# Modulation rows in the weight-sum tiles, one a pair, and chunk 0 of the key and value activations prepared beside the query pairs

## The chip, the core and the metric

The kernel runs on one core of a Trainium2 chip. The core has five engines with instruction queues of their own: TensorE (PE in the profile, its weight loads are PEld), VectorE (DVE), ScalarE (ACT), GpSimd (POOL) and SyncE (SP, which here only issues DMAs). Each queue is worked off in order; an instruction whose semaphore is not there yet holds all behind it. The metric is the device time of one execution in microseconds. Three timed runs of the kernel before gave 2887.72, 2887.82 and 2893.54 us, median 2887.82.

## The reference

A decoder trunk of two layers on `x` (1024 tokens by 1024 channels, float32). Layer 0 mixes by causal pooling, layer 1 by dilated attention over keys and values projected from the stream after layer 0. Each layer ends in a gated FFN (1024 to 2 x 2816, a causal convolution over three tokens, SiLU gate, 2816 to 1024). Every sub-layer is normalised, scaled and shifted by modulation rows, and added back through a gate row. What matters here:

```python
cond = jax.nn.silu(c)
mod = cond @ ada_w[layer] + ada_b[layer]              # six rows of 1024 a layer
sh1, sc1, g1, sh2, sc2, g2 = jnp.split(mod, 6, axis=-1)
...
kv_shift, kv_scale = jnp.split(cond @ kv_ada_w + kv_ada_b, 2, axis=-1)
hkv = _modulate(_rmsnorm(x, kv_norm_g), kv_shift, kv_scale)
kv = (hkv @ w_kv).reshape(b, s, 2, N_BRANCHES, N_HEADS, HEAD_DIM)
...
h = _modulate(_rmsnorm(x, norm2_g[layer]), sh2, sc2)
x = x + g2[:, None, :] * _conv_ffn(h, ...)
```

So a modulation row of 1024 values is a product of a vector with a 1024 x 1024 matrix: 14 of them, 4 MB each.

## The kernel before

Activations lie transposed in SBUF, channels on partitions, tokens in two chunks of 512. Every float32 operand is split in a high part (written by ScalarE, L107, `whi`, `h`, `slab`) and a low part (VectorE subtracts, L108, `wlo`, `l`), and a product is three matmuls: high by high, high by low, low by high (L341 to L343, L415 to L417, L1012 to L1014).

The up projection of an FFN and the query projection run in **pairs** (`Pair`, 22 in an FFN, 12 for the queries) by a scheme of seven products of 2 x 2 blocks. For a pair, VectorE forms weight sums in two tiles of a pool `s` that has two places: `s21` (L455, L456) and `s34` (L460, L461), which are then split. The first eight pairs have two of their products made ahead and parked in DRAM (`ed`, L436); `rest` loads them back. `gate` (L492) evacuates the products, convolves (L504), and stores the row to `gd` by a DMA from GpSimd's queue (L533).

The down projection (`Ffn.down`, L549) goes through the 22 rows of `gd` in sets of three, the last of four. Each set loads its rows and weights through three places `wraw`, splits them, and walks eight row blocks by two chunks (`down_pieces`); VectorE adds each result to the stream tile `x` (L377). The last set (`down_last`, L382) also norms: chunk 0 is finished first, then `steps(0)` is advanced once per piece of chunk 1: its first step makes `nps` on TensorE, the square root chain and the diagonal `ndg` on VectorE (L207), the second the broadcast `nrs` on TensorE (L210), and the others scale one row block each (L222, L228). It has four call sites, one for each norm joint of the kernel: into the first FFN, into the query projection, into the second FFN, and into the output.

Modulation rows 0 to 4 are made early in other ways. Rows 5, 6, 7, 12, 13 come from `ada_dot` (L317) in the first FFN, rows 8 to 11 in the value projection: eight tiles `araw` of 512 KB a row are loaded by SyncE, multiplied by the broadcast `condr` on GpSimd (L324), and summed by four accumulating copies each on ScalarE (L327). `bg_ada` calls it a whole row at a time, behind pair 12 and between the sets of the down projection.

After the pairs of the query projection, `hkx` (L991 to L993) loads the stream of both chunks back, scales and shifts it for keys and values (`hk`), and the value projection follows in 12 groups `cg` with results `vps`.

Outside an early hand-ordered stretch and the attention, the order on each queue is not that of the code: a scheduler puts every instruction where its own timing model thinks it is ready, within the places that tile pools leave. What the code fixes is which tile an operation uses and which it must wait for.

Of the kernel before, what the change touches and what calls it, by code (L numbers as in the profile page):

```python
# [9 lines left out]
F32 = mybir.dt.float32  # L10
# [8 lines left out]
KT = 8  # L19
# [10 lines left out]
LEAD = 2  # L30
# [27 lines left out]
def trunk(ctx, tc, xT, prm, cvec, ada_w, ada_t, pw_in, pgrp, pw_out, wk, wv, wq, wo, wup, wdn, out):  # L58
# [258 lines left out]
    def ada_dot(i, tp, condr):  # L317

        q = cp.tile([128, 8, KQ], F32, tag="q", bufs=1, name=nm("q"))
        for m in range(8):  # L320
            raw = tp.tile([128, 1024], F32, tag="t4", name=nm("araw"))
            o = D * (i - 5) + 128 * m
            nc.sync.dma_start(raw, ada_t[o:o + 128, :])
            nc.gpsimd.tensor_tensor(raw, raw, condr, op=ALU.mult)  # L324
            w = D // KQ
            for k in range(KQ):
                nc.scalar.activation(raw[:, w * k:w * k + w], raw[:, w * k:w * k + w], AF.Copy,  # L327
                                     accum_out=q[:, m, k:k + 1])

        def fin():  # L330
            nc.vector.reduce_sum(mod(i), q, axis=mybir.AxisListType.X)
            nc.vector.tensor_add(mod(i), mod(i), ada_bias(i))
        return fin
# [48 lines left out]
    def down_last(ga, gb, x, g, norm, done):  # L382


        down(*gb, x, g, (0,), norm)

        def steps(c):
            r = norm.rstd(c)
            next(r)
            yield  # L390
            yield from done(c, next(r))

        ap = steps(0)
        for m, _ in enumerate(down_pieces(ga[0] + gb[0], ga[1] + gb[1], x, g, (1,), norm)):
            if m in (0, 1) or m >= LEAD:
                next(ap)
        for _ in ap:
            pass
        return steps(1)
# [86 lines left out]
    class Ffn:  # L486
# [49 lines left out]
        def up(self, late, bg={}):  # L536
# [7 lines left out]
            for i, p in enumerate(ps):  # L544
                p.rest(self.gate(i))
                if i in bg:
                    bg[i]()

        def down(self, norm, done, bg=()):  # L549
# [6 lines left out]
            for n, tags in enumerate(sets):  # L556
# [333 lines left out]
    fins = []  # L890

    def bg_ada(i):

        for i0, f0 in fins:
            f0()
            if i0 in scales:
                scaleg(i0, scales[i0])
        fins[:] = [(i, ada_dot(i, tp, condr))] if i is not None else []

    def bg_ada_list(ids):  # L900
        return [lambda i=i: bg_ada(i) for i in ids]

# [5 lines left out]

    f0 = Ffn(0, tp, hs1, SL0, xd[0], gd[0])

    def first_ada():
        nonlocal condr
        condr = load_condr()
        bg_ada(5)

    condr = None
    f0.up(late, {12: first_ada, 17: lambda: bg_ada(None)})
    x, late = f0.down(nrm, done1, bg_ada_list((6, 7, 12, 13, None)))
# [55 lines left out]
    if True:  # L974
# [12 lines left out]
        hk = Hid((Q[2], Q[4], Q[3], Q[5], Q[6], Q[7], Q[8], Q[9]))  # L987
        for c in range(2):
            for ft in range(KT):
                t = tp.tile([128, 512], F32, tag="t2", name=nm("hkx"))  # L990
                nc.sync.dma_start(t, xd[1][128 * ft:128 * ft + 128, 512 * c:512 * c + 512])  # L991
                nc.vector.scalar_tensor_tensor(t, t, mod(13)[:, ft:ft + 1], rms[c], op0=ALU.mult, op1=ALU.mult)  # L992
                nrm.parts(t, mod(12)[:, ft:ft + 1], hk.g(c, 0, ft), hk.g(c, 1, ft))  # L993

        condr = load_condr()
# [404 lines left out]
```

## Time and profile before

| | |
|---|---|
| three timed runs | 2887.72, 2887.82, 2893.54 us |
| the profiled execution | 2893.38 us, its span 2891.6 us |
| TensorE busy | 2732.7 us, 95% of the span |
| VectorE, ScalarE, GpSimd busy | 63%, 41%, 19% |
| granted TensorE clock, mean | 0.974 |
| pairs of the first FFN (from the last `ed` store to the last product) | 332.83 to 763.90 us |
| the same in the second FFN | 2248.76 to 2626.42 us |
| value projection starts | 1242.4 us |

The kernel is near the busy time of TensorE, so the shares of the page say little; what can be won stands in the stretches where TensorE waits or its clock is granted at less than 1. A window row gives, for a stretch, the busy time of each engine and how many instructions it ran: two stretches with the same matmuls can be set side by side. The first and the second FFN are such a pair.

### The profile page before, as it was taken

The page shows a single profiled execution, that of the slowest core. Times are in us where ns is not written, and L with a number is a line of the kernel's source. Part 1 is how long each engine was busy: PE and PEld are TensorE (multiplying, and loading weights), DVE is VectorE, ACT ScalarE, POOL GpSimd, SP SyncE. Part 2 cuts the span into 40 slices and gives each one's busy share as a digit, 9 for nine tenths or more (in the row PEclk, how much of TensorE's full clock was granted, in tenths as well). Part 3 has the DMA queues.
Part 4 walks back from the last instruction along what each step waited for, and adds up shares of the span by engine and source line. Part 5 has one row for each costly group of instructions (what it writes and reads, how often), then busy time and mean ns, then how long its engine had stood idle before and what let it go on. Part 6 is the DMA issues. An engine that isn't in the chain of part 4 may idle for free.

```text
span 2891.6 us, 38074 instructions
## 1 busy us (share of the span) xinstructions
PE 2732.7 (95%) x14220; PEld 2243.5 (78%) x14220; DVE 1832.1 (63%) x3215; ACT 1195.5 (41%) x2599; POOL 548.2 (19%) x454
## 2 busy tenths in 40 slices
PE   7989988899999999989999999999989999999997
PEld 4767766688888788879998777777667888888885
DVE  6897899866655576551113555556668886666554
ACT  4634656644311342354423444445345444443112
POOL 2475154400000200024300222222142000000001
PEclk9998999999999999999999999999999999999998
DMA  7434555422532245465432333333433432225221
GB/s 286 160 100 162 178 210 174 152 87 88 196 110 95 79 168 206 130 237 201 161 102 82 97 97 98 112 97 118 134 103 137 143 123 85 87 88 211 88 73 59
DMA packets 148825, 384.29 MB, mean 133 GB/s; under 512 B 15536, under 2 KB 53408, under 8 KB 148640
## 3 DMA queue, kind: packets, MB, share of 16 engines
q1 hardware_dynamic: 109872, 292.90, 30.3%
q10 hardware_dynamic: 26496, 50.34, 4.8%
q0 software_dynamic: 12272, 38.62, 4.1%
q8 instruction: 112, 1.84, 0.3%
q14 instruction: 73, 0.60, 0.1%
HBM read 295.75 MB, written 86.05 MB: 132 GB/s over the span
## 4 chain that ended last, share of the span: by engine, by line
PE 68%; DVE 14%; DMA 8%; issue 6%; ACT 3%; POOL 2%; SPq 0%; ACTq 0%; DVEq 0%; POOLq 0%
PE pX L415 7%; PE pX L416 6%; PE pX L417 6%; PE dps L341 6%; PE dps L342 6%; PE dps L343 6%; PE vps L1014 3%; PE vps L1013 3%; PE vps L1012 3%; PE pY L415 3%; PE pY L417 3%; PE pY L416 3%; DVE at L504 2%; PE kps L341 2%; PE kps L343 1%
## 5 line engine op out<-in xcount | busy, mean ns | idle before, releaser
L108 DVE TENSOR_TENSOR wlo<-wraw,whi 128x1024 fp32r<-128x1024 f32 x164 | 214.1, 1313 | 295.1 <-ACT whi L107 292.8
L341 PE MATMUL dps<-slab,whi 128*128 128x512 f32 x832 | 330.5, 399 | 6.9 <-DVE x L377 5.3
L342 PE MATMUL dps<-slab,whi 128*128 128x512 f32 x832 | 327.5, 395 | 0.0
L343 PE MATMUL dps<-slab,wlo 128*128 128x512 f32 x832 | 325.1, 394 | 2.3 <-DVE wlo L108 2.3
L377 DVE SCALAR_TENSOR_TENSOR x<-dps,mods,x 128x512 f32<-128x512 f32 x280 | 203.3, 746 | 157.8 <-PE dps L343 153.4
L107 ACT ACTIVATE whi<-wraw 128x1024 fp32r<-128x1024 f32 x164 | 170.1, 1053 | 302.0 <-PE dps L342 190.5
L324 POOL TENSOR_TENSOR araw<-araw,condr 128x1024 f32<-128x1024 f32 x72 | 187.7, 2616 | 479.1 <-DVE hkx L992 249.6
L1185 ACT ACTIVATE ss<-ss,ngm 128x128 f32<-128x128 f32 (+1 forms) x384 | 168.1, 439 | 191.8 <-DVE ngm L1182 180.7
L1012 PE MATMUL vps<-whi,h 128*128 128x256 f32 x768 | 218.5, 285 | 9.0 <-ACT h L227 8.9
L1014 PE MATMUL vps<-whi,h 128*128 128x256 f32 x768 | 217.6, 285 | 5.1 <-DVE h L228 5.0
L1013 PE MATMUL vps<-wlo,h 128*128 128x256 f32 x768 | 217.6, 284 | 0.0
L341 PEld LDWEIGHTS dps<-slab,whi 128*128 128x128 f32 x832 | 159.1, 191 | 44.7 <-DVE x L377 8.3
L415 PE MATMUL pX<-ht,whi 128*128 128x512 f32 x448 | 177.3, 396 | 16.6 <-ACT at L521 8.7
L343 PEld LDWEIGHTS dps<-slab,wlo 128*128 128x128 f32 x832 | 159.0, 191 | 36.7 <-DVE wlo L108 2.8
L342 PEld LDWEIGHTS dps<-slab,whi 128*128 128x128 f32 x832 | 159.2, 191 | 33.8 <-issue 1.0
L416 PE MATMUL pX<-ht,whi 128*128 128x512 f32 x448 | 175.9, 393 | 0.0
L417 PE MATMUL pX<-ht,wlo 128*128 128x512 f32 x448 | 174.9, 392 | 0.0
L107 ACT ACTIVATE whi<-s 128x1024 fp32r<-128x1024 f32 x112 | 118.1, 1057 | 113.5 <-PE pY L416 60.2
L341 PE MATMUL kps<-h,whi 128*128 128x512 f32 x384 | 164.6, 429 | 0.0
L504 DVE SCALAR_TENSOR_TENSOR at<-at,P 128x512 f32<-128x512 f32 (+2 forms) x176 | 156.2, 894 | 8.2 <-ACT at L501 6.7
L1012 PEld LDWEIGHTS vps<-whi,h 128*128 128x128 f32 x768 | 148.4, 193 | 10.0 <-ACT h L227 10.0
L1014 PEld LDWEIGHTS vps<-whi,h 128*128 128x128 f32 x768 | 147.5, 193 | 6.3 <-DVE h L228 6.2
(256 smaller groups left out, 6596.6 us busy)
## 6 DMA issues: line engine op xcount, KB each, us to landing
wraw<-in_wup_dram SPq DMA_DIRECT2D x104, 512.0 KB, 3.7
araw<-in_ada_t_dram SPq DMA_DIRECT2D x72, 512.0 KB, 4.0
gd<-at POOLq DMA_DIRECT2D x44, 512.0 KB, 3.7
wraw<-gd SPq DMA_DIRECT2D x44, 512.0 KB, 3.5
wraw<-in_wdn_dram SPq DMA_DIRECT2D x44, 512.0 KB, 4.1
wraw<-in_wq_dram SPq DMA_DIRECT2D x32, 512.0 KB, 3.9
xd<-x ACTq DMA_DIRECT2D x48, 256.0 KB, 2.0
ed<-ah ACTq DMA_DIRECT2D x24, 512.0 KB, 2.9
```

Of the source, the lines that this page charges most:

```text
L107: nc.scalar.activation(hi, raw, AF.Copy)
L108: nc.vector.tensor_tensor(lo, raw, hi.bitcast(F32), op=ALU.subtract)
L341: nc.tensor.matmul(ps, whi, hhi, start=first, stop=False)
L342: nc.tensor.matmul(ps, whi, hlo, start=False, stop=False)
L343: nc.tensor.matmul(ps, wlo, hhi, start=False, stop=last)
L415: nc.tensor.matmul(ps, w[0][:, k], hh, start=start and j == 0, stop=False, **kw)
L416: nc.tensor.matmul(ps, w[0][:, k], hl, start=False, stop=False, **kw)
L417: nc.tensor.matmul(ps, w[1][:, k], hh, start=False, stop=j == 3, **kw)
L504: nc.vector.scalar_tensor_tensor(t[:, lo + o:hi], a[:, lo + o - d:hi - d], pc(cw, 22 * (2 - d) + i), t[:, lo + o:hi], op0=ALU.mult, op1=AL ...
L1012: nc.tensor.matmul(o, a, whi[:, k], start=kt == 0, stop=False)
L1013: nc.tensor.matmul(o, a, wlo[:, k], start=False, stop=False)
L1014: nc.tensor.matmul(o, b, whi[:, k], start=False, stop=kt == KT - 1)
```

## The change

Three edits.

First, `ada_dot` becomes a generator that does one tile of a row a step, in a pool whose name is passed. In the first FFN its tiles take a place of the pool `s`, the one of the weight sums, and not one of `t4`. One step is made behind each of pairs 8 to 17 (the first of them only loads `condr`), and up to six between the pieces of each set of the down projection. In the value projection four steps are made at each group from group 2 on.

Second, for chunk 0 of the key and value activations the stream is loaded into two free tiles `hx` and scaled there ahead of query pair 9 in the code, and shifted and split behind the last pair; the tiles `hk` are put in another order so that chunk 0 takes those whose last reader is the begin of the last pair. Chunk 1 stays as it was.

Third, the constant `LEAD` goes, and `down_last` does not advance the norm at piece 1, so all but its first step come one piece later, at all four joints.

```diff
-    def ada_dot(i, tp, condr):
+    def ada_dot(i, tp, condr, tag):
...
-            raw = tp.tile([128, 1024], F32, tag="t4", name=nm("araw"))
+            raw = tp.tile([128, 1024], F32, tag=tag, name=nm("araw"))
...
+            yield
+        nc.vector.reduce_sum(mod(i), q, axis=mybir.AxisListType.X)
...
         for m, _ in enumerate(down_pieces(ga[0] + gb[0], ga[1] + gb[1], x, g, (1,), norm)):
-            if m in (0, 1) or m >= LEAD:
+            if m != 1:
                 next(ap)
...
                 if n < len(sets) - 1:
-                    down(rhs, ws, x, mod(6 * l + 5))
-                    if n < len(bg):
-                        bg[n]()
+                    for m, _ in enumerate(down_pieces(rhs, ws, x, mod(6 * l + 5))):
+                        if aw is not None and m < 6:
+                            ada_steps(aw, 1)
+            if aw is not None:
+                ada_steps(aw, 99)
...
+    def ada_run(ids, tag):
+
+        condr = load_condr()
+        yield
+        for i in ids:
+            yield from ada_dot(i, tp, condr, tag)
...
-    f0.up(late, {12: first_ada, 17: lambda: bg_ada(None)})
-    x, late = f0.down(nrm, done1, bg_ada_list((6, 7, 12, 13, None)))
+    aw = ada_run((5, 6, 7, 12, 13), "s")
+    f0.up(late, {i: 1 for i in range(8, 18)}, aw)
+    x, late = f0.down(nrm, done1, aw)
...
         for i, p in enumerate(ps_):
+            if i == 9:
+                hx = big.tile([128, 4, 512], F32, tag=Q[2], name="hx0"), big.tile([128, 4, 512], F32, tag=Q[3], name="hx1")
+                for ft in range(KT):
+                    t = hx[ft // 4][:, ft % 4, :]
+                    nc.sync.dma_start(t, xd[1][128 * ft:128 * ft + 128, 0:512])
+                    nc.vector.scalar_tensor_tensor(t, t, mod(13)[:, ft:ft + 1], rms[0], op0=ALU.mult, op1=ALU.mult)
             p.rest(q_out(i))
+        hk = Hid((Q[4], Q[6], Q[5], Q[7], Q[2], Q[3], Q[8], Q[9]))
+        for ft in range(KT):
+            nrm.parts(hx[ft // 4][:, ft % 4, :], mod(12)[:, ft:ft + 1], hk.g(0, 0, ft), hk.g(0, 1, ft))
...
-        bgl = bg_ada_list((8, 9, 10, 11, None))
+        aw = ada_run((8, 9, 10, 11), "t4")
         for cg in range(12):
-            if cg % 2 == 0 and cg < 10:
-                bgl[cg // 2]()
+            if cg >= 2:
+                ada_steps(aw, 4)
```

How the instructions move, at three places. SyncE's queue in the early pairs of the first FFN, before (`wraw` are weights, `p` and `at` parts made ahead, `araw` modulation tiles):

```order
L323 DMA araw_3944<-in_ada_t_dram 128x1024
L103 DMA wraw_2757<-in_wup_dram 128x1024
L323 DMA araw_3951<-in_ada_t_dram 128x1024
L446 DMA p_373_2550<-ed 128x512
L446 DMA p_388_2655<-ed 128x512
L323 DMA araw_3958<-in_ada_t_dram 128x1024
L323 DMA araw_3965<-in_ada_t_dram 128x1024
L323 DMA araw_3972<-in_ada_t_dram 128x1024
L103 DMA wraw_2762<-in_wup_dram 128x1024
L323 DMA araw_3979<-in_ada_t_dram 128x1024
```

The same queue in the changed kernel, in pairs 9 to 12, where its first `araw` stand:

```order
L102 DMA wraw_3557<-in_wup_dram 128x1024
L322 DMA araw_3548<-in_ada_t_dram 128x1024
L102 DMA wraw_3589<-in_wup_dram 128x1024
L102 DMA wraw_3696<-in_wup_dram 128x1024
L322 DMA araw_3687<-in_ada_t_dram 128x1024
L102 DMA wraw_3728<-in_wup_dram 128x1024
L102 DMA wraw_3835<-in_wup_dram 128x1024
L322 DMA araw_3826<-in_ada_t_dram 128x1024
```

Before, all 40 tiles of the first FFN were multiplied ahead of the 11th of the 22 `gd` stores on GpSimd's queue. Now none stands in the eight pairs with parts made ahead, nine stand behind these, one between the two weight loads of a pair, and 31 stand in the last two pairs and the down projection, among its loads.

VectorE's queue at the second norm joint (into the query projection), before:

```order
L174 TENSOR_TENSOR nv_6906<-nv_6906 128x4
L207 TENSOR_SCALAR ndg_6914<-ident,nv_6906 128x128 x4
L222 SCALAR_TENSOR_TENSOR x_5190<-x_5190,mods,rs_6938 128x512
L222 SCALAR_TENSOR_TENSOR x_5191<-x_5191,mods,rs_6938 128x512
L222 SCALAR_TENSOR_TENSOR x_5192<-x_5192,mods,rs_6938 128x512
```

and now:

```order
L173 TENSOR_TENSOR nv_6906<-nv_6906 128x4
L206 TENSOR_SCALAR ndg_6914<-ident,nv_6906 128x128 x4
L376 SCALAR_TENSOR_TENSOR x_5200<-dps_6936,mods,x_5200 128x512
L221 SCALAR_TENSOR_TENSOR x_5198<-x_5198,mods,rs_6956 128x512
L221 SCALAR_TENSOR_TENSOR x_5199<-x_5199,mods,rs_6956 128x512
```

One more piece of the projection (`dps`, 12 matmuls on TensorE) stands between the diagonal and what uses its broadcast.

TensorE's queue where the value projection starts, before (`pX` belongs to the last query pair):

```order
L416 MATMUL pX_8655<-ht_7450,h_1294_8697 128x512
L417 MATMUL pX_8655<-ht_7449,l_1295_8698 128x512
L1012 MATMUL vps_8946<-whi_8935,h_8785 128x256
L1013 MATMUL vps_8946<-wlo_8936,h_8785 128x256
L1012 MATMUL vps_8996<-whi_8935,h_8785 128x256
```

and now, with three of the last pair's seven products still behind these rows:

```order
L416 MATMUL pY_8719<-ht_7449,wlo_8706 128x512
L1012 MATMUL vps_8880<-whi_8869,h_8792 128x256
L1013 MATMUL vps_8880<-wlo_8870,h_8792 128x256
L1012 MATMUL vps_8930<-whi_8869,h_8792 128x256
L1013 MATMUL vps_8930<-wlo_8870,h_8792 128x256
L414 MATMUL pX_8673<-ht_7180,whi_8711 128x512
```

The first values of chunk 0 have moved in among the products of the last pair. The eight scalings of `hx` themselves have moved further: the scheduler has put them beside the evacuations of query pair 0.

## Rows read from the trace of the kernel before

**Rows 1.** Page, busy time: busy us, share of the span, instructions

```profile
PE 2732.7 (95%) x14220; PEld 2243.5 (78%) x14220; DVE 1832.1 (63%) x3215; ACT 1195.5 (41%) x2599; POOL 548.2 (19%) x454
```

**Rows 2.** Windows: us, each engine's busy us (instructions), TensorE clock, DMA share, GB/s

```profile
332.80:763.90 431.10, 393.74 (x1662) 319.24 (x1661) 343.96 (x395) 227.91 (x539) 119.86 (x61) 0.96 0.44 148
2248.80:2626.40 377.60, 376.59 (x1661) 311.50 (x1661) 279.43 (x383) 165.00 (x218) 11.26 (x21) 1.00 0.33 113
763.90:987.30 223.40, 220.15 (x980) 182.50 (x978) 123.08 (x158) 44.11 (x48) 4.39 (x4) 1.00 0.34 116
```

**Rows 3.** Timeline of ScalarE's queue, last `ed` store of each FFN: start us, us

```profile
332.83 0.33 ACTq L436 DMA_DIRECT2D ed<-ah  x1
...
2248.76 0.33 ACTq L436 DMA_DIRECT2D ed<-ah  x1
```

**Rows 4.** Timeline of TensorE, last product of the last pair of each FFN

```profile
763.90 0.39 PE L417 MATMUL pX<-ht,l 128*128 128x512 f32 x1
...
2626.42 0.39 PE L417 MATMUL pX<-ht,l 128*128 128x512 f32 x1
```

**Rows 5.** Groups of VectorE by form, 343 to 563 us: busy us, mean ns

```profile
L504 DVE SCALAR_TENSOR_TENSOR at<-at,P 128x510 f32<-128x510 f32 x12 | 17.3, 1446 | 0.0
...
L525 DVE TENSOR_TENSOR at<-pY,at 128x512 f32<-128x512 f32 x11 | 7.5, 680 | 1.1 <-PE pY L417 1.1
```

**Rows 6.** Groups of VectorE by form, 2258 to 2445 us

```profile
L504 DVE SCALAR_TENSOR_TENSOR at<-at,P 128x510 f32<-128x510 f32 x13 | 9.6, 743 | 0.1
...
L525 DVE TENSOR_TENSOR at<-pY,at 128x512 f32<-128x512 f32 x12 | 8.2, 687 | 11.8 <-PE pY L417 11.8
```

**Rows 7.** Tile `araw`: duration ns min/median/max; landing of its loads

```profile
L327 ACT ACTIVATE araw<-araw x288: 397/402/426, 348.0 to 1426.7; 128x256 f32<-128x256 f32 x144
...
L324 POOL TENSOR_TENSOR araw<-araw,condr x72: 2354/2411/3527, 343.9 to 1420.6; 128x1024 f32<-128x1024 f32 x72
...
DMA to landing us min/median/max: 3.3/4.0/8.3
```

**Rows 8.** Timeline of VectorE in one pair of the second FFN

```profile
2457.07 0.68 DVE L108 TENSOR_TENSOR l<-wraw,h 128x512 fp32r<-128x512 f32 x1
...
2461.70 0.69 DVE L455 TENSOR_TENSOR s<-wraw 128x512 f32<-128x512 f32 x1 [1.37 <-DMA wraw<-in_wup_dram]
...
2462.31 0.68 DVE L460 TENSOR_TENSOR s<-wraw,wraw 128x512 f32<-128x512 f32 x1
...
2466.43 0.69 DVE L523 TENSOR_TENSOR v<-pX,v 128x512 f32<-128x512 f32 x1 [1.10 <-PE pX L417]
```

**Rows 9.** Timeline of TensorE, `nrs` of chunk 0 at the four norm joints: idle before

```profile
260.00 1.66 PE L210 MATMUL nrs<-ndg,ones 128*128 128x512 f32 x2 [3.38 <-DVE ndg L207]
...
987.31 1.07 PE L210 MATMUL nrs<-ndg,ones 128*128 128x512 f32 x1 [3.26 <-DVE ndg L207]
...
2175.21 1.12 PE L210 MATMUL nrs<-ndg,ones 128*128 128x512 f32 x1 [3.46 <-DVE ndg L207]
...
2849.04 1.22 PE L210 MATMUL nrs<-ndg,ones 128*128 128x512 f32 x1 [2.48 <-DVE ndg L207]
```

**Rows 10.** Windows at and behind the start of the value projection

```profile
1242.40:1290.00 47.60, 33.57 (x242) 31.52 (x242) 33.22 (x32) 26.95 (x77) 20.29 (x8) 0.93 0.70 252
1290.00:1337.60 47.60, 47.60 (x399) 47.60 (x399) 9.41 (x11) 26.85 (x91) 21.18 (x9) 1.00 0.65 220
```

**Rows 11.** Timeline of SyncE's queue at the start of the value projection

```profile
1240.72 4.01 SPq L991 DMA_DIRECT2D hkx<-xd  x6
```

**Rows 12.** Timeline of VectorE there, first `hkx`

```profile
1246.54 0.75 DVE L992 SCALAR_TENSOR_TENSOR hkx<-hkx,mods,rs 128x512 f32<-128x512 f32 x1 [4.49 <-DMA hkx<-xd]
```

**Rows 13.** Timeline of VectorE, first evacuations of the first down projection

```profile
769.03 1.41 DVE L377 SCALAR_TENSOR_TENSOR x<-dps,mods,x 128x512 f32<-128x512 f32 x2 [1.52 <-DMA x<-xd]
```

**Rows 14.** Windows in the query pairs

```profile
1070.00:1080.00 10.00, 10.00 (x46) 8.29 (x45) 4.40 (x6) 1.69 (x2) 0.00 (x0) 1.00 0.16 60
```

More of the change, by code (lines that the diff above doesn't have):

```diff
@@ L29 @@
 RATE = 2.5
-LEAD = 2
 KQ = 4
@@ L328, in ada_dot @@
                                      accum_out=q[:, m, k:k + 1])
[L330 to L333, printed above, removed]
+            yield
+        nc.vector.reduce_sum(mod(i), q, axis=mybir.AxisListType.X)
+        nc.vector.tensor_add(mod(i), mod(i), ada_bias(i))
+        if i in scales:
+            scaleg(i, scales[i])
     def scaleg(i, gname):
@@ L534, in gate, with up @@
             return evac
-        def up(self, late, bg={}):
+        def up(self, late, bg={}, aw=None):
             ps = [Pair(wup[self.l][i], wup[self.l][NF + i], self.ops, self.tp) for i in range(NF)]
@@ L546, in up, with down @@
                 if i in bg:
-                    bg[i]()
-        def down(self, norm, done, bg=()):
+                    ada_steps(aw, bg[i])
+        def down(self, norm, done, aw=None):
             l = self.l
@@ L889, in trunk @@
     scales = {7: "n1_1", 13: "kvn", 10: "n2_1"}
[L890 to L901, printed above, removed]
     def load_condr():
@@ L907, in load_condr, with ada_steps @@
         return t
-    f0 = Ffn(0, tp, hs1, SL0, xd[0], gd[0])
[L911 to L916, printed above, removed]
-    f0.up(late, {12: first_ada, 17: lambda: bg_ada(None)})
-    x, late = f0.down(nrm, done1, bg_ada_list((6, 7, 12, 13, None)))
+    def ada_run(ids, tag):
[3 more added lines that the diff above has]
+            yield from ada_dot(i, tp, condr, tag)
+    def ada_steps(a, n):
+        for _ in range(n):
+            next(a, None)
+    f0 = Ffn(0, tp, hs1, SL0, xd[0], gd[0])
+    aw = ada_run((5, 6, 7, 12, 13), "s")
+    f0.up(late, {i: 1 for i in range(8, 18)}, aw)
+    x, late = f0.down(nrm, done1, aw)
     def perm_view(ap, g, c=None):
@@ L983, in trunk @@
         for i, p in enumerate(ps_):
+            if i == 9:
[4 more added lines that the diff above has]
+                    nc.vector.scalar_tensor_tensor(t, t, mod(13)[:, ft:ft + 1], rms[0], op0=ALU.mult, op1=ALU.mult)
             p.rest(q_out(i))
+        hk = Hid((Q[4], Q[6], Q[5], Q[7], Q[2], Q[3], Q[8], Q[9]))
+        for ft in range(KT):
+            nrm.parts(hx[ft // 4][:, ft % 4, :], mod(12)[:, ft:ft + 1], hk.g(0, 0, ft), hk.g(0, 1, ft))
         st0.close()
         st0, tp = temps("tv")
[L987 to L995, printed above, removed]
-        bgl = bg_ada_list((8, 9, 10, 11, None))
+        for ft in range(KT):
+            t = tp.tile([128, 512], F32, tag="t2", name=nm("hkx"))
+            nc.sync.dma_start(t, xd[1][128 * ft:128 * ft + 128, 512:1024])
+            nc.vector.scalar_tensor_tensor(t, t, mod(13)[:, ft:ft + 1], rms[1], op0=ALU.mult, op1=ALU.mult)
+            nrm.parts(t, mod(12)[:, ft:ft + 1], hk.g(1, 0, ft), hk.g(1, 1, ft))
+        aw = ada_run((8, 9, 10, 11), "t4")
         for cg in range(12):
-            if cg % 2 == 0 and cg < 10:
-                bgl[cg // 2]()
+            if cg >= 2:
+                ada_steps(aw, 4)
             w = [wprep(wv[cg, i]) for i in range(2)]
```

## The prediction

> **What bounds the kernel now.** I read the page first: TensorE is busy 2732.7 of 2891.6 us [rows 1], so at most 159 us can be won by taking waits away, and the shares say nothing of where. Then windows over the stages, because the kernel holds its own control: the second FFN does the same work as the first and computes no modulation rows. From the last parked part [rows 3] to the last product of the last pair [rows 4], the first FFN takes 431.1 us and the second 377.6, for 1662 and 1661 matmuls [rows 2]. The 53.5 us between them are what 40 modulation tiles cost there. Next the engines of these two windows: VectorE 64.5 us more, ScalarE 62.9, GpSimd 108.6, which is 1.6, 1.6 and 2.7 us a tile. The mechanism is in the groups by form: the convolution step, which reads two tensors of SBUF, takes 1446 ns in the first FFN and 743 in the second, while the addition that reads one operand from PSUM takes 680 and 687 [rows 5, 6]. So VectorE is held while GpSimd multiplies, in the pairs where it has least to spare, and TensorE waits for it. Two other places show waits: the start of the value projection, where 47.6 us hold 242 matmuls against 399 in the next 47.6 [rows 10], a loss of 157/399 x 47.6 = 18.7 us; and the broadcast of chunk 0 at each norm joint, 3.38, 3.26, 3.46 and 2.48 us, 12.6 in all [rows 9]. The three edits stand at these three places; together they can give back at most 53.5 + 18.7 + 12.6 = 84.8 us.
>
> **The pairs of the first FFN.** No instruction is added or removed; 40 tiles are moved. The eight pairs with parked parts get none and should run as in the second FFN. Nine tiles follow, one a pair. What is new is a wait: the tile takes one of the two places of `s`, so the next pair's `s34` must wait until it is loaded, multiplied and summed. I follow it in one pair of the second FFN [rows 8]. SyncE issues the tile behind a weight load that waits for the split `l`, which ends at 2457.75. From there: 4.0 us to land, 2.41 for the multiplication, 4 x 0.40 for the copies [rows 7], with the issues about 8.5, so 2466.2. The sum `s34` (L460) began at 2462.31; it comes 3.9 us late. Behind it on VectorE stands the evacuation L523, which began at 2466.43 after 1.10 us of idle: it slips by some 0.5 to 1 us, and TensorE has the fourth block's 12 matmuls (2.7 us at 377.6/1661 each) to do before it needs that bank. So it is hidden. As a loop: 8.5 us of chain, then ten VectorE instructions up to the next `l`, some 7.5 us at about 0.75 each, and up to 1.6 for the multiplication; 17.6 in a pair of 19.1 us (84 matmuls). With a load at its longest, 8.3, and a multiplication of 3.53 [rows 7], it would be 23, over by 4. I take 5 us lost over the nine pairs: a gain of 48, bounds 53.5 (none lost) and 53.5 - 9 x 4 = 17.
>
> The row says that VectorE loses 1.6 us a tile. The Trainium skill (SBUF — State Buffer, Who interferes with whom) says that a VectorE instruction with two SBUF inputs and a GpSimd one that reads SBUF exclude each other for the whole instruction, whichever starts first. The trace agrees on who is hit (1446 against 680 ns), and the rule adds the other direction: the multiplication may stand behind VectorE's work and lengthen the loop. By the longest multiplication, 3.53 us, on all nine the loop is 18.7 us, still under 19.1; by rule and long loads together it is R1 below.
>
> **The down projection.** It takes the other 31 tiles. Its window is full of TensorE work, 220 of 223.4 us, with VectorE 123, ScalarE 44, GpSimd 4 [rows 2]. Adding 31 x 1.6 to VectorE and ScalarE and 31 x 2.7 to GpSimd gives 173, 94 and 88: all still under 223. Two places of `s` with a chain of about 8.3 us deliver a tile each 4.2; the code wants one each 223.4 x 3/22/6 = 5.1. So they fit. What can be late: SyncE's queue now holds tiles between the loads of `x`, and already the first evacuation waited 1.52 us for `x` [rows 13]. Eight PSUM banks stand against that. I take 3 us; bounds 0 and 31 x 1.34 = 42 (53.5/40 a tile, as in the pairs), nearest to the row of the same stage with its slack, so near 0.
>
> **The start of the value projection.** Before, the first `hkx` load is issued at 1240.72 [rows 11], the first scaling starts at 1246.54 [rows 12], and TensorE has nothing else. Now chunk 0 is split during the last pair, and 74 of the first group's 96 chunk-0 matmuls are left behind it, by the order: 74 x 47.6/399 = 8.8 us of cover. Chunk 1 needs 5.8 us to the first scaling and then 8 x 1.5 us on VectorE, 17.8 us from its issue. TensorE takes its eight row blocks one by one, 12 matmuls or 1.4 us each, so it follows at VectorE's pace and ends some 5 us behind a full one. Gain 18.7 - 5 = 13; bounds 8 (no overlap of the blocks) and 18.7.
>
> The scalings of `hx` go to query pair 0: 8 x 0.75 = 6 us of VectorE beside its evacuations, just ahead of a stretch where VectorE is busy 4.4 of 10 us [rows 14]. 1 us, bounds 0 and 6.
>
> **The norm joints.** With 24 in place of 12 matmuls between `nps` and `nrs`, each wait loses at most 2.7 us: 2.7 + 2.7 + 2.7 + 2.5 = 10.6. `nrs` comes at the same absolute time, for VectorE's chain sets it, so the scaling behind it is no later, apart from one evacuation (0.7 us) now between. At the first joint the sums of rows 3 and 4 also change place. I take 9, bounds 0 (what follows waits as long as before) and 12.6.
>
> **Sum.** 48 - 3 + 13 - 1 + 9 = 66 us. The profiled execution took 2893.4 us, so its like would be 2827. It stands 5.6 us over the median of the runs, 2887.8, of which two lie at 2887.7 and 2887.8; against that median the forecast is 2822 us. Were all the bounds good, 2803; the terms at 35 (the middle of the pairs' bounds), -3, 8, -3 and 0 give 37 us or 2851.
>
> **Rivals.**
> R1, the two places of `s` bind the pairs: the loop is over 19.1 us with loads of 5.5 us or more or multiplications that stand behind VectorE, and each microsecond over costs nine. For it: the loop has only 1.5 us to spare, and three loads are issued together. Against: VectorE has idle time to take it up, and 4.0 us is the median of the 72 loads of before, with DMA busier in the pairs than it need be now (0.44 against 0.33 in the second FFN [rows 2]). At 3 us over, 27 are lost: 66 + 5 - 27 = 44, so 2844.
> R2, the down projection is paced by its tiles, and it ends slower than before: SyncE works in order, so a tile that waits for its place holds the weights behind it. It decides from a chain of 10.2 us (two places, 5.1 us a tile); at 16 us a tile comes each 8.0, and 31 x (8.0 - 5.1) = 90 us are lost: 2822 + 90 = 2912. For it: the longest load and multiplication make 8.3 + 3.5 + 1.6 = 13.4. Against: those are maxima, and the medians make 8.0.
> R3, the value projection only swaps its wait: chunk 1 becomes as late as chunk 0 was, 14.7 us are lost instead of 18.7, and the term is 4: 2831. For it: only 8.8 us of cover. Against: eight loads in place of sixteen and no multiplications beside them.
> R4, the joints give nothing, since GpSimd's squares bind what follows: 2831.
>
> **Chances and range.** A result within 0.2% (5.8 us) of before cannot be told from no change. Forecast 0.70, R1 0.12, R2 0.03, R3 0.08, R4 0.07. Faster: all but R2 and a rest in which several terms fail at once, 0.95; within 0.2%: 0.02; slower 0.03. The range is 2806 (nearly all the losses gone) to 2851 (the low sum above); it takes in R1, R3 and R4.
>
> **What would show it.** In the changed profile the window from the last parked part to the last product should be near 380 us, with no group of VectorE in the first eight pairs above its duration in the second FFN. If L459 of pairs 10 to 18 is late and the evacuations behind it are waited for, R1 is at work. In the down projection TensorE should stay full at clock 1.00; waits for `wlo` or for evacuations behind `x` loads would be R2. At the value projection, TensorE's waits should name chunk 1's `h` alone and sum to about 5 us. `nrs` of chunk 0 should wait under 1 us at all four joints. The forecast is wrong if the window of the pairs is over 400 us, or that of the down projection over 235.

## The result, and the profile after

The changed kernel takes 2825.6 us in the median of four runs (2813.58 to 2827.43), the kernel before 2890.1 beside it: a ratio of 0.9767, 95% interval 0.9737 to 0.9797. Run again beside the experiments it gave 0.9770 (0.9757 to 0.9784). The forecast was 2822. The profiled execution took 2824.1 us, its span is 2822.4, so the two profiled executions differ by 69.3 us where the sum said 66. The total was right to 4 us, but its terms were not: the value projection and the joints are off by 4 us or more, in opposite directions.

Line numbers of the changed kernel are one lower than before, up to the code of the FFN. The page's busy line, as in [rows 1]:

```profile
PE 2712.8 (96%) x14220; PEld 2233.7 (79%) x14220; DVE 1795.5 (64%) x3215; ACT 1197.4 (42%) x2599; POOL 552.8 (20%) x454
```

Windows, with columns as in [rows 2]: the pairs of the first FFN, the down projection up to the first `nps` of the norm joint, and the pairs of the second FFN; then 47.6 us from the first `vps` and the 47.6 behind them, which answer to [rows 10]:

```profile
332.70:714.20 381.50, 378.54 (x1668) 312.51 (x1668) 298.74 (x383) 188.78 (x345) 56.70 (x38) 1.00 0.40 134
714.20:935.50 221.30, 216.41 (x944) 177.49 (x942) 135.50 (x156) 82.08 (x238) 65.56 (x28) 0.99 0.50 173
2184.30:2561.60 377.30, 376.86 (x1662) 311.56 (x1662) 279.94 (x383) 165.85 (x218) 11.26 (x21) 1.00 0.33 113
1190.00:1237.60 47.60, 47.60 (x365) 46.06 (x364) 20.75 (x26) 14.47 (x20) 0.00 (x0) 1.00 0.59 201
1237.60:1285.20 47.60, 47.60 (x399) 47.60 (x398) 7.65 (x4) 22.60 (x71) 16.88 (x7) 1.00 0.57 183
```

The pairs went from 431.1 to 381.5 us and are 4.2 us from the second FFN. Of the 49.6 us won there, 34.4 are idle time of TensorE (37.4 before, 3.0 now) and 15.2 are busy time, 393.7 against 378.5 us for about the same matmuls, with the granted clock up from 0.96 to 1.00. The value projection starts without a wait: TensorE is busy for all of its first 47.6 us. (The first window holds 365 and not 399 matmuls because some are still the longer ones of the last query pair.) The window of the down projection has 4.9 us of idle TensorE (2.6 for `whi`, 1.2 for `wlo`, 1.1 for the stream `x`), and it had none before:

```profile
763.90:979.50 215.60, 215.60 (x954) 178.53 (x952) 119.71 (x146) 41.47 (x44) 4.39 (x4) 1.00 0.35 118
```

Cutting both executions at the same events gives the whole account. The cuts are the last `ed` store [rows 3], the last product of the pairs [rows 4], the first `nps` of each joint, the `nrs` of chunk 1, and the last `vps`:

| stretch | before, us | after | gain | forecast |
|---|---|---|---|---|
| pairs of the first FFN | 431.1 | 381.5 | 49.6 | 48 |
| down projection to the first `nps` | 215.6 | 221.3 | -5.7 | -3 |
| joint into the query projection, to `nrs` of chunk 1 | 44.0 | 44.0 | 0.0 | joints together 9 |
| query pairs and value projection | 514.1 | 495.4 | 18.7 | 13 - 1 |
| attention, to the first `nps` | 629.7 | 628.0 | 1.7 | none |
| joint into the second FFN | 44.2 | 44.1 | 0.1 | in the 9 |
| second FFN, to the first `nps` of the last joint | 630.6 | 630.2 | 0.4 | none |
| last joint to the end | 49.6 | 45.2 | 4.4 | in the 9 |

The first joint lies in the stretch to the last `ed` store, 332.8 and 332.7 us; from its first `nps` to that store it is 84.4 and 83.6.

VectorE's groups in the first pairs of the first FFN (343 to 448 us, ahead of the first tile) stand where [rows 6] had them, not where [rows 5] had them:

```profile
L503 DVE SCALAR_TENSOR_TENSOR at<-at,P 128x510 f32<-128x510 f32 x8 | 5.9, 746 | 0.0
...
L524 DVE TENSOR_TENSOR at<-pY,at 128x512 f32<-128x512 f32 x8 | 5.5, 687 | 0.0
```

One later pair with a tile shows what is left of the interference. A timeline row gives start and duration in us, and in brackets the engine's idle time before it and what ended it. VectorE first, then GpSimd, then SyncE's queue:

```profile
552.75 1.23 DVE L107 TENSOR_TENSOR wlo<-s,whi 128x1024 fp32r<-128x1024 f32 x1 [0.17 <-ACT whi L106]
...
558.21 2.45 DVE L531 TENSOR_TENSOR at<-at,v 128x512 f32<-128x512 f32 x1
...
560.58 0.68 DVE L107 TENSOR_TENSOR l<-wraw,h 128x512 fp32r<-128x512 f32 x1
...
566.06 0.70 DVE L454 TENSOR_TENSOR s<-wraw 128x512 f32<-128x512 f32 x1 [4.14 <-DMA wraw<-in_wup_dram]
566.67 0.68 DVE L459 TENSOR_TENSOR s<-wraw,wraw 128x512 f32<-128x512 f32 x1
...
557.72 2.39 POOL L323 TENSOR_TENSOR araw<-araw,condr 128x1024 f32<-128x1024 f32 x1 [15.21 <-DVE at L503]
...
554.05 0.33 SPq L322 DMA_DIRECT2D araw<-in_ada_t_dram  x1
```

The tile lands 3.5 us after its issue, and the multiplication begins 0.17 us later, at 557.72 (the row's bracket names L503, but it was the load that came). The product L531, which reads two tensors of SBUF, then takes 2.45 us in place of 0.69 (683 ns in the second FFN). That is 1.8 us of VectorE, and six of the nine pairs with a tile have it at this product. The cost is still paid, but in slack. The 4.1 us in which VectorE waits for weights are not this slack, since their load is issued behind the split `l` that stands behind L531. It is VectorE's wait for TensorE's products: 4.7 us in these six pairs, 27.5 in the same stretch of the second FFN, and TensorE is full in both:

```profile
495.00:609.00 114.00, 114.00 (x504) 94.43 (x503) 85.34 (x104) 57.05 (x115) 17.88 (x12) 1.00 0.34 107
2347.00:2461.00 114.00, 114.00 (x505) 94.42 (x504) 76.09 (x102) 48.96 (x66) 3.19 (x6) 1.00 0.25 84
```

At the norm joints [rows 9] each `nrs` of chunk 0 indeed waits less (the first still 2.43 us); but at the second and third joint a new wait appears behind it:

```profile
259.57 1.22 PE L209 MATMUL nrs<-ndg,ones 128*128 128x512 f32 x1 [2.43 <-DVE ndg L206]
...
943.44 1.13 PE L209 MATMUL nrs<-ndg,ones 128*128 128x512 f32 x2 [0.54 <-DVE ndg L206]
...
965.06 0.50 PE L414 MATMUL pX<-hb,whi 128*128 128x512 f32 x1 [4.17 <-ACT ah L432]
...
2110.86 1.13 PE L209 MATMUL nrs<-ndg,ones 128*128 128x512 f32 x2 [0.54 <-DVE ndg L206]
...
2132.48 0.50 PE L414 MATMUL pX<-hb,whi 128*128 128x512 f32 x1 [4.17 <-ACT ah L432]
...
2785.09 1.12 PE L209 MATMUL nrs<-ndg,ones 128*128 128x512 f32 x2 [0.54 <-DVE ndg L206]
```

`ah` is the evacuation of a part made ahead. On ScalarE it stands behind the high parts `hb`, and these wait for the scalings of every second row block on GpSimd, one piece later than before:

```profile
946.08 6.86 POOL L218 TENSOR_TENSOR x<-x,rs 128x512 f32<-128x512 f32 x4
952.93 8.01 POOL L219 TENSOR_SCALAR x<-x,mods 128x512 f32<-128x512 f32 x4
960.91 4.39 POOL L194 TENSOR_TENSOR sq<-sq,sq 128x512 f32<-128x512 f32 x2
...
963.83 0.70 ACT L226 ACTIVATE hb<-x,mods 128x512 fp32r<-128x512 f32 x1
964.44 0.57 ACT L432 ACTIVATE ah<-pX 128x512 f32<-128x512 f32 x1
```

GpSimd works without a gap from 946.1 to 965.3, so by the trace it sets this joint now; no run took that work away. In the kernel before, TensorE's second wait at this joint was another one, 2.31 us for a sum of squares on GpSimd:

```profile
1011.44 0.59 PE L202 MATMUL nps<-ones,sq 128*128 128x1 f32 x2 [2.31 <-POOL sq L195]
```

The waits of the joint add up to 5.7 us before and 5.5 now, and the stretch stays at 44.0 us.

The last joint has no projection behind it, and there the wait had cost more than itself. Windows just behind the `nrs`, before and after (columns as in [rows 2]):

```profile
2850.20:2854.20 4.00, 4.00 (x10) 2.81 (x9) 2.42 (x2) 1.32 (x2) 2.37 (x2) 0.50 0.00 0
```

```profile
2786.30:2790.30 4.00, 4.00 (x19) 3.33 (x18) 3.36 (x3) 1.33 (x3) 3.81 (x3) 1.00 0.02 6
```

After the wait of 2.48 us before, the granted clock was 0.50, the lower of the two levels, and TensorE did 10 matmuls in 4 us. Now it does 19 at clock 1.00. How long the clock stays low is not the same in every run: 6.8 us in the kernel before and in `e2` below, 3.4 us in `e1`, `e4` and `e11` behind the same wait of 2.48 us. Their last joint takes 47.3 us where the kernel before takes 49.6, so part of the 4.4 us is the clock of one execution.

### The profile page after: what moved, and what is told of

Its sections match the earlier page's. It is cut to its first block, busy times and chain, and to the rows that moved or that the text cites. A ratio compares the mean times of both kernels' runs of the same rounds, so it can differ in the third digit from the quotient of the medians.

```text
span 2822.4 us, 38016 instructions
## 1 busy us (share of the span) xinstructions
PE 2712.8 (96%) x14220; PEld 2233.7 (79%) x14220; DVE 1795.5 (64%) x3215; ACT 1197.4 (42%) x2599; POOL 552.8 (20%) x454
## 4 chain that ended last, share of the span: by engine, by line
PE 70%; DVE 8%; DMA 8%; issue 5%; POOL 2%; ACT 2%; SPq 0%; ACTq 0%; DVEq 0%; POOLq 0%
PE pX L414 8%; PE pX L415 8%; PE pX L416 8%; PE dps L340 5%; PE dps L341 5%; PE dps L342 5%; PE pY L414 3%; PE pY L416 3%; PE pY L415 3%; PE vps L1014 3%; PE vps L1013 3%; PE vps L1012 3%; PE kps L340 2%; DMA araw<-in_ada_t_dram 2%; PE kps L342 2%
## 5 line engine op out<-in xcount | busy, mean ns | idle before, releaser
L107 DVE TENSOR_TENSOR wlo<-wraw,whi 128x1024 fp32r<-128x1024 f32 x164 | 229.8, 1409 | 306.9 <-ACT whi L106 304.2
L326 ACT ACTIVATE araw<-araw 128x256 f32<-128x256 f32 x288 | 116.4, 405 | 113.2 <-POOL araw L323 110.8
L342 PE MATMUL kps<-h,wlo 128*128 128x512 f32 x384 | 152.3, 397 | 0.0
L1178 DVE CUSTOM_DVE_ANT_0 ss<-sc,bias 128x128 f32<-128x128 f32 (+1 forms) x384 | 111.2, 345 | 64.6 <-PE sc L1172 64.3
```

Of the source, the lines that this page charges most:

```text
L107: nc.vector.tensor_tensor(lo, raw, hi.bitcast(F32), op=ALU.subtract)
L342: nc.tensor.matmul(ps, wlo, hhi, start=False, stop=last)
```

## The experiments

The pieces of the change alone come first, then what the account left open. Times are compared with runs of the kernel before on the same chip.

**One edit at a time.** `e1`: the changed kernel with the norm order and the key and value activations of before.

```diff
-            if m != 1:
-                next(ap)
+            next(ap)
...
-        hk = Hid((Q[4], Q[6], Q[5], Q[7], Q[2], Q[3], Q[8], Q[9]))
-        for ft in range(KT):
-            nrm.parts(hx[ft // 4][:, ft % 4, :], mod(12)[:, ft:ft + 1], hk.g(0, 0, ft), hk.g(0, 1, ft))
...
+        hk = Hid((Q[2], Q[4], Q[3], Q[5], Q[6], Q[7], Q[8], Q[9]))
+        for c in range(2):
+            for ft in range(KT):
...
```

> Only the first edit: modulation tiles in the places of the weight sums, one a pair and six a set; the norm order and the key and value activations as before. Theory (each edit acts in its own stretch): pairs of the first FFN about 381 us as in the changed kernel, down projection 6 to 7 us slower, all else as before: 43 us less than before, ratio 0.985. Rival (the edits lean on each other: what the tiles cost in the down projection grows with the norm order of before): gain under 35 us, with the down projection over 10 us slower.

Measured: 0.9811 (0.9788 to 0.9833); cut as above, the pairs take 383.9 us, the down projection 220.3, query pairs and value projection 508.5 in place of 514.1. So the theory holds for the FFN (the down projection loses 4.7 us where it said 6 to 7) and the rival falls. What neither foresaw is that the first edit also wins 5.5 us in query pairs and value projection: it also makes the tiles of rows 8 to 11 begin at group 2, away from the splits of both chunks. `e4` below, whose tiles are not multiplied at all, has 509.1 there. TensorE's waits in `e1`:

```profile
1206.63 0.58 PE L1004 MATMUL vps<-whi,h 128*128 128x256 f32 x1 [5.48 <-ACT h L226]
1209.54 0.58 PE L1006 MATMUL vps<-whi,h 128*128 128x256 f32 x1 [1.68 <-DVE h L227]
```

`e2`: the kernel before with the second edit alone, both hunks of it.

```diff
+            if i == 9:
+                hx = big.tile([128, 4, 512], F32, tag=Q[2], name="hx0"), big.tile([128, 4, 512], F32, tag=Q[3], name="hx1")
...
+        for ft in range(KT):
+            nrm.parts(hx[ft // 4][:, ft % 4, :], mod(12)[:, ft:ft + 1], hk.g(0, 0, ft), hk.g(0, 1, ft))
...
```

> Only the second edit: chunk 0 of the key and value activations prepared beside the query pairs, with the modulation rows of the first FFN and of the value projection as before (whole rows at groups 0, 2, 4, ..., so the first eight multiplications on GpSimd still stand beside the splits of chunk 1). Theory A (the loss was the serial chain of loads, scalings and splits): gain 18 us, ratio 0.994, no wait of TensorE behind the last query pair. Theory B (half of it came from the multiplications that hold VectorE there): gain 9 to 13 us, with VectorE's scalings of chunk 1 stretched to over 1 us beside the multiplications and TensorE waiting for chunk 1.

Measured: 0.9942 (0.9924 to 0.996), query pairs and value projection 495.7 us, a gain of 18.4, no wait of TensorE: theory A. The window from the first `vps` on:

```profile
1240.80:1288.40 47.60, 47.60 (x366) 46.12 (x365) 21.18 (x26) 23.00 (x63) 16.70 (x7) 1.00 0.74 256
```

There are multiplications in it (16.7 us of GpSimd), but chunk 1 has all of chunk 0's matmuls for cover. So the 5.5 us of `e1` and the 18.4 of `e2` are one loss taken from two sides, not two gains; the changed kernel has 18.7.

`e3`: the kernel before with the third edit alone.

```diff
-            if m in (0, 1) or m >= LEAD:
+            if m != 1:
                 next(ap)
```

> Only the third edit: the norm is not advanced at piece 1 of the last set. Forecast's term: 9 us less, ratio 0.997. Reading of the changed kernel's trace: at joints 2 and 3 the wait of 3.3 us is replaced by a wait for the evacuation of the part made ahead, and about 1 us is left at each, 0.4 at the first; 5 at the last: 7.6 us, ratio 0.9974. Rival R4 (what follows binds at every joint): 0 to 2 us, ratio 0.9993 to 1.

Measured: 0.9977 (0.9962 to 0.9992). The stretches: second joint 43.9 us, third 44.0, last 43.8 in place of 49.6; the waits for `ah` of 4.17 us stand at both middle joints. So R4 holds at the two middle joints, and the last gives most. The first, from its first `nps` to the last `ed` store, takes 82.2 us here; the five kernels without the third edit have 83.5 to 84.8, the eight with it 82.2 to 83.6, so it gives 1.4 us in the mean.

**What held VectorE.** `e4`: the kernel before without the multiplications on GpSimd.

```diff
-            nc.gpsimd.tensor_tensor(raw, raw, condr, op=ALU.mult)
```

> The kernel before with the 72 multiplications by condr on GpSimd left out (the modulation rows 5 to 13 are then plain row sums); loads and accumulating copies stay. Theory (the multiplications hold VectorE in the pairs): the convolution step in the pairs falls from 1446 to about 745 ns a piece, the window from the last parked part to the last product falls from 431 to 378 to 390 us, and the whole kernel gains 40 to 55 us there and a few us at the value projection, ratio 0.98 to 0.985. Rival (ScalarE's 160 accumulating copies, or the 20 MB of loads in the way of weights, make the loss): the window stays above 415 us and VectorE's idle time in it grows instead.

Measured: 0.9796 (0.9776 to 0.9816). The pairs, and the convolution step in the stretch of [rows 5]:

```profile
331.40:716.40 385.00, 380.01 (x1662) 312.22 (x1661) 280.93 (x395) 227.40 (x538) 11.41 (x21) 1.00 0.48 166
```

```profile
L503 DVE SCALAR_TENSOR_TENSOR at<-at,P 128x510 f32<-128x510 f32 x14 | 10.4, 746 | 0.2
```

With the multiplications gone, 46 of the 53.5 us go; all 160 copies and 20 MB of loads together are worth the other 7. VectorE's busy time is that of the second FFN, 281 against 279 us.

**What spreads the tiles.** `e6`: one word of the changed kernel.

```diff
-    aw = ada_run((5, 6, 7, 12, 13), "s")
+    aw = ada_run((5, 6, 7, 12, 13), "t4")
```

> The changed kernel with one word changed: the tiles of the first FFN take the places of t4 again, while the code still asks for one a pair. Theory (the place orders the tiles, not the line of code: the scheduler moves them ahead wherever a place is free): the 40 multiplications stand again in the early pairs, the convolution step there goes back to over 1400 ns, the pairs take 425 to 435 us, and the ratio goes back to about 0.993 to 0.996. Rival (one a pair in the code is enough): pairs 380 to 390 us, ratio 0.977.

Measured: 0.9923 (0.991 to 0.9937). The window of the pairs, and the same group:

```profile
328.40:764.10 435.70, 396.54 (x1658) 319.16 (x1657) 347.48 (x392) 228.48 (x538) 118.33 (x61) 0.96 0.44 146
```

```profile
L503 DVE SCALAR_TENSOR_TENSOR at<-at,P 128x510 f32<-128x510 f32 x12 | 23.2, 1938 | 0.0
```

With the `t4` places the pairs are as slow as before the change (435.7 us), though the code asks for one tile a pair: all 40 are multiplied between 340 and 562 us. The scheduler moves a tile ahead as far as a place is free; only the place that the weight sums hold keeps it in its pair.

**What the down projection loses.** The changed kernel itself, without an edit (`e5`), ran beside `e6` to `e8` as their measure.

> The changed kernel once more, as the measure for the kernels beside it on the same chip. Ratio to before 0.977; pairs of the first FFN 381 us, down projection up to the norm 221 us, query pairs and value projection together 495 us.

Measured: 0.9770 (0.9757 to 0.9784), median 2826.6; pairs 381.4, down 221.2, query and value 495.7 us.

In the trace of the changed kernel TensorE waits for `whi` at 781.40. SyncE had five tiles in line from 763.48, with a load of a row of `gd` behind them; that was R2 in small, and the first suspect. The rows of TensorE, ScalarE and SyncE's queue:

```profile
781.40 0.79 PE L340 MATMUL dps<-slab,whi 128*128 128x512 f32 x1 [2.35 <-ACT whi L106]
...
778.69 0.42 ACT L326 ACTIVATE araw<-araw 128x256 f32<-128x256 f32 x1 [3.73 <-POOL araw L323]
...
780.30 2.94 ACT L106 ACTIVATE whi<-wraw 128x1024 fp32r<-128x1024 f32 x3
...
763.05 0.33 SPq L102 DMA_DIRECT2D wraw<-in_wdn_dram  x1
763.48 17.30 SPq L322 DMA_DIRECT2D araw<-in_ada_t_dram  x5
782.63 0.33 SPq L102 DMA_DIRECT2D wraw<-gd  x1
```

`e7` takes the tiles out of that queue:

```diff
-            nc.sync.dma_start(raw, ada_t[o:o + 128, :])
+            nc.gpsimd.dma_start(raw, ada_t[o:o + 128, :])
```

> The changed kernel with the loads of the modulation tiles issued by GpSimd's queue in place of SyncE's. Theory (the down projection loses its 5.7 us because tiles that wait for a place hold the weights behind them in SyncE's queue, R2 in small): down projection 215 to 217 us with no wait of TensorE for whi; 4 to 6 us less than the changed kernel, ratio to it 0.998 to 0.9985. Rival A (ScalarE and VectorE are the late ones, with the sums of the tiles among the splits): down projection stays at 220 to 222. Rival B (the loads on GpSimd's queue hold the gd stores behind them): the first loads of gd come late and the down projection takes 225 us or more.

Measured: 0.9777 (0.9764 to 0.9791), down 223.3 us, between what rivals A and B said. The suspect falls. (The trace above says so too: the weights issued at 763.05 land 3.9 us later, 13 us before ScalarE's copies at 780.30.) TensorE's longest wait, and ScalarE just before it:

```profile
812.77 0.77 PE L340 MATMUL dps<-slab,whi 128*128 128x512 f32 x1 [4.96 <-ACT whi L106]
...
810.06 0.42 ACT L326 ACTIVATE araw<-araw 128x256 f32<-128x256 f32 x1 [4.56 <-POOL araw L323]
...
811.68 1.04 ACT L106 ACTIVATE whi<-wraw 128x1024 fp32r<-128x1024 f32 x1
```

ScalarE stood idle for 4.56 us before the copies of a tile that GpSimd had not multiplied yet, with `whi` behind them. The changed kernel has the same at 778.69, 3.73 us of idle, and `whi` at 780.30. So ScalarE is late, as rival A had it, but not because it is busy: it is held at the head of its queue.

`e8` moves the multiplication to VectorE:

```diff
-            nc.gpsimd.tensor_tensor(raw, raw, condr, op=ALU.mult)
+            nc.vector.tensor_tensor(raw, raw, condr, op=ALU.mult)
```

> The changed kernel with the multiplication of the 72 tiles by condr on VectorE in place of GpSimd: no operation of GpSimd stands beside VectorE's there. Theory (the two exclude each other, and a multiplication on GpSimd costs VectorE 1.6 us, what it takes itself for 1024 elements): VectorE's busy time stays within 20 us of the changed kernel's 1795, pairs 380 to 385 us, down 219 to 223, total within 6 us of the changed kernel. Rival (GpSimd's work is mostly beside VectorE's, and only 20 or 30% is paid): VectorE's busy time rises by 70 us or more and the total by over 6 us.

Measured: 0.9757 (0.9743 to 0.977), median 2822.7. Page's busy line, and the windows of pairs and down projection:

```profile
PE 2711.3 (96%) x14220; PEld 2232.5 (79%) x14220; DVE 1831.1 (65%) x3287; ACT 1198.4 (42%) x2599; POOL 366.1 (13%) x382
```

```profile
332.10:709.30 377.20, 377.11 (x1664) 311.93 (x1663) 293.96 (x398) 187.55 (x344) 11.41 (x21) 1.00 0.41 134
709.30:929.30 220.00, 215.08 (x946) 177.16 (x945) 148.41 (x180) 84.03 (x239) 4.40 (x4) 1.00 0.51 176
```

VectorE's busy time rose by 36 us, between theory and rival: it now does 72 multiplications of 1.22 us, 88 us, so by this difference those on GpSimd had cost it 52, or 0.7 us each in the changed kernel. The pairs reach the second FFN's 377 us. The down projection still waits 4.4 us for `whi`, and ScalarE again stands idle ahead of the copies, 3.3 and 3.4 us at 771.14 and 807.64, now for VectorE's multiplication.

`e9` takes ScalarE out as well:

```diff
-            nc.gpsimd.tensor_tensor(raw, raw, condr, op=ALU.mult)
-            w = D // KQ
-            for k in range(KQ):
-                nc.scalar.activation(raw[:, w * k:w * k + w], raw[:, w * k:w * k + w], AF.Copy,
-                                     accum_out=q[:, m, k:k + 1])
+            nc.vector.scalar_tensor_tensor(raw, raw, 1.0, condr, op0=ALU.mult, op1=ALU.mult,
+                                           accum_out=q[:, m, 0:1])
...
```

> The changed kernel with a tile's multiplication (GpSimd) and its four accumulating copies (ScalarE) replaced by one VectorE instruction that multiplies and accumulates. Theory after the loads on GpSimd's queue did not help (whi stands in ScalarE's queue behind the copies of a tile that is not yet multiplied, and TensorE waits for it): with no copy on ScalarE, whi comes in time, the down projection takes 215.6 to 217 us as before the change, the pairs 377 to 379 as with the multiplication on VectorE, and the total is 4 to 6 us under the 2822.7 of the multiplication on VectorE: 2816 to 2819, ratio to before 0.974. Rival (SyncE's queue holds the weights behind tiles that wait for their place): the two places and the queue are as they were, so down stays at 219 to 222. Rival (VectorE, which now waits itself for a tile's load with the low parts of the weights behind it): waits for wlo, down 220 or more.

Measured: 0.9729 (0.9713 to 0.9744), median 2817.0, the lowest of all, as forecast from the theory. TensorE's only wait over 0.25 us in the down projection is 0.6 us for the stream `x`, with tiles and weights still in one queue of SyncE:

```profile
331.20:710.40 379.20, 379.01 (x1671) 313.07 (x1670) 297.01 (x421) 163.27 (x217) 11.44 (x21) 1.00 0.41 136
710.40:924.40 214.00, 213.25 (x940) 175.93 (x939) 145.20 (x198) 43.61 (x46) 4.40 (x4) 1.00 0.51 176
```

`e9` also shortens the time for which a tile holds its place. That the waiting copies are the cause, and not this, rests on the rows of ScalarE above and on `e7`.

**Are the two places near their limit?** `e10` doubles the tiles in the pairs.

```diff
-    f0.up(late, {i: 1 for i in range(8, 18)}, aw)
+    f0.up(late, {i: 1 if i == 8 else 2 for i in range(8, 18)}, aw)
```

> The changed kernel with two tiles in place of one behind each of pairs 9 to 17: 18 tiles in the pairs, 22 left for the down projection. The prediction's loop (two places of s shared by s21, s34 and the tile, chain of a tile 8.5 us, 17.6 of 19.1 us used): a second tile adds 8.5 us, or 4.3 if the two lie beside each other in the two places, so the loop is 22 to 26 us, 3 to 7 us over in each of nine pairs: pairs 405 to 440 us, ratio 0.986 or more. Rival (the places are not near their limit, since the chain lies beside VectorE's work): pairs 382 to 390 us, and the total within 5 us of the changed kernel.

Measured: 0.9749 (0.9734 to 0.9764), median 2821.1; pairs 384.0 us, and the down projection, with 22 tiles in place of 31, 215.5, what it took before the change. The loop of the prediction falls. The sum L459 does wait for the tile's copies now, 8.3 us in nine pairs (500 to 700 us), but TensorE does not wait in these pairs before 694 us:

```profile
L459 DVE TENSOR_TENSOR s<-wraw,wraw 128x512 f32<-128x512 f32 x9 | 6.2, 691 | 8.3 <-ACT araw L326 8.3
```

**The place or the engine?** `e11`: the kernel before, its 40 tiles still in the early pairs, with the instruction of `e9`.

> The kernel before, with its placing of the tiles as it was (all in the early pairs), but the multiplication and the copies replaced by one VectorE instruction of about 1.2 us a tile. If what the pairs lost was VectorE's time (1.6 us a tile through the multiplications on GpSimd, against 1.2 for its own): VectorE still has 49 us more to do in the early pairs and the window stays at 405 to 425 us, ratio 0.990 to 0.993. If it was the exclusion itself, a VectorE instruction held for up to 2.4 us at a moment when TensorE needs it: 378 to 390 us, ratio 0.979 to 0.983.

Measured: 0.9841 (0.9825 to 0.9857), pairs 402.1 us, between the two expectations. The window, and the new instruction in the stretch of [rows 5]:

```profile
331.30:733.40 402.10, 385.54 (x1663) 314.85 (x1662) 323.58 (x475) 165.06 (x218) 11.44 (x21) 0.98 0.48 159
```

```profile
L324 DVE SCALAR_TENSOR_TENSOR araw<-araw,condr 128x1024 f32<-128x1024 f32 x40 | 48.3, 1215 | 1.0 <-DMA araw<-in_ada_t_dram 1.0
```

So with the multiplications off GpSimd and the copies off ScalarE, 29 of the 53.5 us go and 24.5 stay, with 48.3 us of VectorE still in the pairs where it has no slack. Spreading them (`e9`) brings another 22.9.

## Why the prediction was right, and where it was not

**The pairs: right, by a chain that started at the wrong time.** 49.6 us against 48. The cause was as read: the second FFN as control gave 53.5 us to win, and `e4` and `e6` show multiplications and their place to be what cost it. But the loop argument was wrong. The chain was sized right: from the issue at 554.05 to the end of the copies at 562.2 it takes 8.2 us, and I had 8.5. Its start was not: I let SyncE issue the tile at the end of the split `l`, when the sums of the same pair are due. In the trace the tile is issued at 554.05, as soon as a place is let go by the split of a weight sum (`s` into `wlo`, which ends at 553.98, some 12 us behind `l`), and it is done 4.4 us ahead of the next L459 at 566.67. The sum is not 3.9 us late, and R1, to which I gave 0.12 and 27 us, was not near; `e10` with twice the tiles loses 2.5 us. That 5 us were taken and 4.2 lost is luck: the loss stands elsewhere, 3.0 of it in waits of 1.08 and 1.88 us in the last 20 us of the pairs, beside the tiles and loads of the down projection that have been moved there.

**The rule of the Trainium skill** (SBUF — State Buffer, Who interferes with whom) was used for its second direction, the multiplication that stands behind VectorE. The pair above shows only the first: L531 starts half a microsecond into the multiplication and ends 0.55 us behind it (560.66 against 560.11). An earlier pair shows both, VectorE first, then GpSimd:

```profile
481.91 1.22 DVE L107 TENSOR_TENSOR wlo<-s,whi 128x1024 fp32r<-128x1024 f32 x1
483.05 2.88 DVE L503 SCALAR_TENSOR_TENSOR at<-at,P 128x511 f32<-128x511 f32 x1
...
482.42 2.96 POOL L323 TENSOR_TENSOR araw<-araw,condr 128x1024 f32<-128x1024 f32 x1 [13.95 <-DMA araw<-in_ada_t_dram]
```

The multiplication starts inside a split and takes 2.96 us in place of 2.39; the convolution step behind the split takes 2.88 in place of 0.75. It did not lengthen the loop, since the loop had room.

**The down projection: right sign, size off.** 5.7 us lost where I took 3. The step that fails is "so they fit": I compared busy times and the rate of the places. What I had not asked is what stands behind a waiting copy on ScalarE. Its queue is in order, and `whi` of the next set stands there. Loads late behind SyncE's queue, which I named as R2, are not the cause (`e7`, `e9`).

**The value projection: too low.** I took 13 of 18.7 us, because TensorE would follow chunk 1 at VectorE's pace; all 18.7 came, with nothing to be seen of the scalings of `hx`. Chunk 1 came no earlier than counted: its first load was issued at 1194.41, its last block was split at 1216.3, 21.9 us later. The 5 us do not follow even from the forecast's own figures: a last block split 17.8 us behind its issue is in time for a TensorE that has 8.8 us of cover and seven blocks of 1.4 us ahead of it, 18.6. And the step that fails is the cover, 74 matmuls of the first group's chunk 0 counted from the end of the last pair. The first load was issued 6.8 us ahead of that, so the cover from its issue was 15.6 us: chunk 1's first matmul starts at 1210.05, and the last block, split at 1216.3, is first used at 1219.9. TensorE's queue has still more: among chunk 1 of the first group (`vps_1326`, with `h_1304` and `h_1305`) the scheduler put chunk 0 of the second group (`vps_1335`, with `h_1300` to `h_1303`), another 96 matmuls that were ready. No run shows whether TensorE would have waited without them. In the order of the queue, three rows of that place:

```
L1012 MATMUL vps_1326_8982<-whi_1317_8869,h_1304_8796 128x256
...
L1013 MATMUL vps_1335_9096<-wlo_1330_9086,h_1300_8792 128x256
...
L1013 MATMUL vps_1326_8982<-wlo_1321_8876,h_1305_8797 128x256
```

I had read the order only up to the end of the first group's chunk 0.

**The norm joints: wrong at three of four.** I took 9 of 12.6; by the table 4.6 came, 4.4 of them at the last. The step that fails is "the scaling behind it is no later, apart from one evacuation". At the middle joints GpSimd's scalings begin with `rs`, and now have one sum of squares ahead of them; the wait only changed its name, from `nrs` and `nps` to `ah`. That is R4, which I had at 0.07, with GpSimd's scalings, by the trace, in the place of its squares. At the last joint I undersized: 2.5 for the wait, and not the matmuls at clock 0.50 behind it.

So the sum was right because two misses cancel: -4.4 (joints) and -2.7 (down projection) stand against +6.7 (value projection and `hx`) and +1.6 (pairs). The remaining 2.1 us lie in the attention and the second FFN, which the change does not touch.

## What to carry to other kernels

A piece of background work is put in its place by the buffer that it must wait for, not by the line of code that asks for it, where a scheduler sets the order (`e6`): look at which pool holds it back. Price work on GpSimd beside VectorE by VectorE's slack at that moment, for the same multiplication cost 1.6 us of VectorE in the crowded pairs and 0.7 when spread; where VectorE can do the whole job in one instruction of 1.2 us, GpSimd and ScalarE are freed and no split of weights stands behind a waiting copy. And when a wait is taken away, name the engine that is next before the gain is booked: at the middle joints it was, by the trace, GpSimd's scalings, which the profile before already shows.

## What the runs showed of the hardware

In `e9` a VectorE instruction that multiplies two 128 x 1024 float32 tensors of SBUF and accumulates took 1.22 us (and 83 ns to read the sum), no more than the plain subtraction of the same size, 1.22 us. On ScalarE the same tile took 1.7 us (four copies of 0.40 with a read of 0.19 behind each, which overlaps with the next copy), on GpSimd 2.4. A multiplication on GpSimd and a VectorE instruction with two SBUF inputs held each other up in either order in the changed kernel (2.96 us against 2.39, 2.45 against 0.69). And a wait of 2.5 us of TensorE at the last joint went with a granted clock of 0.50 for 6.8 us in the kernel before, 5.5 of them behind the wait, so that it cost about twice itself; in `e1`, `e4` and `e11` it was low for 3.4 us. At the two middle joints taking away such a wait won nothing.
